# An opening with sums ahead of factors, and a second sweep whose weights are split two products ahead

## The chip, the cores and the metric

The kernel runs on one core of a Trainium2 chip. The metric is the time of one execution on the device in microseconds (us). The core has a matrix engine (PE), a vector engine (DVE), a scalar engine (ACT) and GpSimd (POOL); SP issues most loads. Each engine executes its own instructions in a fixed order and waits where an operand isn't there.

## The reference

One block of a streaming encoder, in float32, for 1024 tokens of 2048 channels:

```python
mod = einsum('bd,de->be', silu(c), w_ada) + b_ada          # shift, scale, gate
h = rms_norm(x, g_pre) * (1 + scale) + shift
q, f, i, z, bb, cc, vb, zb = split(einsum('bsd,de->bse', h, w_in))   # 8 x 1024 columns
f = lb + (1 - lb) * sigmoid(f); k = 1 - f
o = hgrn2_chunkwise(q, log(f), k, i)       # 8 heads of 128, chunks of 64 tokens
y_a = rms_norm(o, g_head_a) * silu(z)
y_b = bb * causal_conv(cc * vb, conv_w, conv_b) * silu(zb)          # 3 taps
m_a, m_b = split(sigmoid(einsum('bsd,de->bse', h, w_merge) + b_merge))
out = einsum('bse,ed->bsd', m_a * (y_a @ w_up_a) + m_b * (y_b @ w_up_b), w_o)
x + gate * rms_norm(out, g_post)
```

## The kernel before

Every large matrix product is done by Strassen's scheme in Winograd's form: seven products p1 to p7 in place of eight, on sums of blocks. Each operand is split into a high and a low float32r half (`hi` on ACT, `lo = raw - hi` on DVE), and each block product is three matmuls (lines 118, 121, 122: hi hi, hi lo, lo hi). A product of the two sweeps has 8 factors, so 24 matmuls of 128x128 by 128x512.

**Opening.** x is loaded, normalised and transposed. Then for four pairs of factors (q = 0 to 3) `ada_pair(q)` loads 16 blocks of w_ada and sums them weighted with silu(c): the scale on PE, the shift on DVE (`row_v`, 16 operations). `factors_a` then applies scale and shift to the transposed x (ACT), forms p1, p6, p2 and p7's right factors and splits them (tiles `fp`, lines 134 and 135).

**First sweep** (`unit_a`, 48 units: 8 heads of 4, then 16 of gates): products p1, p6, p2, p7 of each unit. Partial sums go to DRAM (`u_scr`, `s_scr`). `factors_b`, `gate_step` and `sums_o` are strewn in.

**Second sweep** (`unit_b`, 48 units): p5, p4, p3 of each unit. A head's units bring q and f, v and z, bb and cc, vb and zb. Behind each unit stands the work that its results allow: `Head.f` (Sigmoid, Ln, scans, four Exp), `q`, `v`, `z`, `scores`, `k_nat`, `states`, `o`, `conv` and `norm` (whose Ln and Exp stand on lines 583 and 587). y of each branch goes to `y_scr`.

**up_b, up_a, out.** `up` forms the factors of y (`yp`, 28 of them), and does 8 steps (`du`) of seven products with 4 factors each. Then the last product with w_o.

The program's order is set by a list scheduler that runs when the kernel is built: it takes the text as priority, and puts each engine's instructions in the order in which its own model has them ready. Tiles are taken from pools: `wp` (`w_hi`, `w_lo` two buffers each, raw weights five), `big` (38 tiles of 512 KB) and a pool for the phase, `ph0` to `ph4`; a phase's tiles lie where those of the phase before lay, and wait for their last use.

Of the kernel before, what the change touches and what calls it, by code (L numbers as in the profile page):

```python
# [26 lines left out]
def tile_hgrn2_shortconv_block(  # L27
# [288 lines left out]
    def unit_a(u):  # L316
        view, e1, e2 = units[u]
        a11, a21 = load_q(view, 0, e1), load_q(view, 0, e2)
        a22, a12 = load_q(view, 1, e2), load_q(view, 1, e1)
        o = ph.tile([P, 3, HS], F32, tag="o", name="o", bufs=2)  # L320
        s1, s2, s4 = (ph.tile([P, 8, P], F32, tag=f"s{n}", name=f"s{n}") for n in (1, 2, 4))
        px, py = ps("mm", "px"), ps("mm", "py")
        product(px, split_w(a11), fa["p1"], pin=u == 0)
# [56 lines left out]
    for u in range(NU):  # L380
        unit_a(u)
        if u < 8:
            factors_b(u)
        elif u < 40:
            gate_step(u - 8)
        else:
            sums_o(u - 40)
# [11 lines left out]
    d_ring = []  # L399
    d_n = [0]  # L400

    def d_tile():
# [4 lines left out]
        return t

    def unit_b(u):
# [8 lines left out]
        pz, pw = ps("mm", "pz"), ps("mm", "pw")  # L418
        product(pz, split_w(s1), fb["p5"])
        nc.vector.tensor_add(out=d2[:, hi_h], in0=d2[:, lo_h], in1=pz)  # L420
        product(pw, split_w(a22), fb["p4"])
        nc.vector.tensor_sub(out=d2[:, lo_h], in0=d2[:, lo_h], in1=pw)
        product(pz, split_w(s4), fb["p3"], more=True)
        nc.vector.tensor_add(out=d1[:, hi_h], in0=d1[:, hi_h], in1=pz)
        return d1, d2
# [42 lines left out]
    class Head:
# [3 lines left out]
        def f(self, sig):  # L472
# [47 lines left out]
        def scores(self):  # L520
            px = [ps("aux", "sc0"), ps("aux", "sc1")]
            for blk in range(8):
                hf, c0 = blk // 4, (blk % 4) * P
                t0, t1 = slice(blk * P, blk * P + CH), slice(blk * P + CH, blk * P + P)
                lo, up = px[hf][0:CH], px[1 - hf][CH:P]
                first, last = blk % 4 == 0, blk % 4 == 3
                nc.tensor.matmul(lo[:, c0:c0 + CH], self.e2[:, t0], self.e1[:, t0], start=first, stop=False, skip_group_check=True)
                nc.tensor.matmul(up[:, c0 + CH:c0 + P], self.e2[:, t1], self.e1[:, t1], start=first, stop=last, skip_group_check=True)
                nc.tensor.matmul(lo[:, c0 + CH:c0 + P], self.e3[:, t0], self.eb[:, t1], start=False, stop=last, skip_group_check=True)
            for hf in range(2):  # L530
                nc.vector.copy_predicated(out=sc_buf[hf][0:CH].rearrange("p a b -> p (a b)"),
                                          mask=cmask[0:CH].rearrange("p a b -> p (a b)"), data=px[hf][0:CH])
# [59 lines left out]
    def conv(ct, d_bb, d_cc, d_vb, d_zb):  # L592
        u = ph.tile([P, S + 2], F32, tag="u", name="u")
        nc.gpsimd.memset(u[:, 0:2], 0.0)
        nc.vector.tensor_mul(out=u[:, 2:S + 2], in0=d_cc, in1=d_vb)
        y = wide("y")
        nc.vector.tensor_scalar(out=y, in0=u[:, 0:S], scalar1=cw_c[:, ct:ct + 1], scalar2=cb_c[:, ct:ct + 1], op0=mult, op1=add)
        for j in (1, 2):
            nc.vector.scalar_tensor_tensor(out=y, in0=u[:, j:j + S], scalar=cw_c[:, j * 8 + ct:j * 8 + ct + 1], in1=y, op0=mult, op1=add)
        nc.vector.tensor_mul(out=y, in0=y, in1=d_bb)  # L600
        nc.vector.tensor_mul(out=y, in0=y, in1=d_zb)
        nc.scalar.activation(out=d_zb, in_=d_zb, func=AF.Sigmoid)
        nc.vector.tensor_mul(out=y, in0=y, in1=d_zb)
        nc.gpsimd.dma_start(out=y_scr[8 + ct], in_=y)

    for i in range(NH):
        hd = Head(i)
        d_q, d_f = unit_b(4 * i)
        hd.f(d_f)
        hd.q(d_q)  # L610
        d_v, d_z = unit_b(4 * i + 1)
        hd.v(d_v)
        hd.z(d_z)
        hd.scores()
        d_bb, d_cc = unit_b(4 * i + 2)
        hd.k_nat()
        hd.states()
        d_vb, d_zb = unit_b(4 * i + 3)
        hd.o()
        conv(i, d_bb, d_cc, d_vb, d_zb)  # L620
        hd.norm()

    for m in range(16):
        for j, t in enumerate(unit_b(32 + m)):
            et = 2 * m + j
            nc.scalar.activation(out=t, in_=t, func=AF.Sigmoid, bias=bm_c[:, et:et + 1])
            nc.gpsimd.dma_start(out=g_scr[et], in_=t)
# [249 lines left out]
```

## Time and profile before

| | us |
|---|---|
| median of 3 runs (lowest, highest) | 2820.7 (2820.16, 2821.09) |
| profiled execution, its span | 2822.96, 2821.3 |
| PE busy | 2668.6 (95%) |
| DVE busy | 1740.5 (62%) |
| ACT busy | 952.8 (34%) |

Busy times of the engines overlap. In the trace the opening lasts to the first matmul of unit 0 at 147 us, the first sweep to 1229, the second to 2160, and the rest to the end. PE's times are those of matmuls in a pipeline, so one matmul's 0.39 us overlaps the next one's. PEclk is the TensorE clock that was granted, as a share of 2.4 GHz.

### The profile page before, as it was taken

Reading aid. Unit: us, or ns where it says so; the run is one execution under the profiler, and the core shown is the slowest. Engines: PE = TensorE matmul, PEld = TensorE weight load, DVE = VectorE, ACT = ScalarE, POOL = GpSimd, SP = SyncE. Lnnn points to the kernel's source line nnn. Section 1 sums busy time; section 2 is a strip of 40 time slices with the busy share of each in tenths; the row PEclk is TensorE's granted clock in tenths of the full one; section 3 lists DMA queues with packets and bytes.
Section 4 is the critical chain, followed back from the end, with each engine's and each line's share of the span. In section 5 each row is a group of like instructions: output and inputs, shape, how many; then the busy total and the mean of one; then the engine's idle time right before and its main releaser. Section 6 shows DMA issues by size and latency. Waiting matters only on the chain.

```text
span 2821.3 us, 31341 instructions
## 1 busy us (share of the span) xinstructions
PE 2668.6 (95%) x11979; PEld 2147.0 (76%) x11979; DVE 1740.5 (62%) x2141; ACT 952.8 (34%) x1208; POOL 241.3 (9%) x430
## 2 busy tenths in 40 slices
PE   6779999999999999999999999999999999999997
PEld 3167787888888888877877777877887877878785
DVE  6778876654554445546556666563338678755668
ACT  5333222222222222234335544434334233232334
POOL 2012111110000000020000000000001101000000
PEclk9789999999999999999999999999999999999999
DMA  9759999985556566683433433447666546672254
GB/s 352 276 192 326 333 346 354 345 277 176 177 194 177 175 174 181 187 293 121 127 123 123 135 127 113 137 160 235 204 207 210 179 142 239 219 278 98 85 213 168
DMA packets 405991, 576.77 MB, mean 204 GB/s; under 512 B 17772, under 2 KB 280016, under 8 KB 405712
## 3 DMA queue, kind: packets, MB, share of 16 engines
q1 hardware_dynamic: 352640, 369.15, 42.4%
q0 software_dynamic: 52016, 201.42, 18.8%
q10 hardware_dynamic: 1184, 4.20, 0.4%
q8 instruction: 94, 1.54, 0.2%
q14 instruction: 57, 0.47, 0.1%
HBM read 405.87 MB, written 168.82 MB: 204 GB/s over the span
## 4 chain that ended last, share of the span: by engine, by line
PE 78%; DVE 8%; ACT 5%; DMA 4%; issue 4%; POOL 1%; DVEq 0%; SPq 0%; POOLq 0%; ACTq 0%
PE po L766 9%; PE py L122 7%; PE py L118 7%; PE py L121 7%; PE px L122 6%; PE px L121 6%; PE px L118 6%; PE pz L118 6%; PE pz L121 6%; PE pz L122 6%; PE pw L122 3%; PE pw L118 3%; PE pw L121 3%; DVE w_lo L130 1%; DMA w_raw<-in_w_in_dram 1%
## 5 line engine op out<-in xcount | busy, mean ns | idle before, releaser
L129 ACT CAST w_hi<-w_raw 128x1024 fp32r<-128x1024 f32 (+1 forms) x304 | 299.3, 985 | 979.1 <-PE px L121 382.8
L130 DVE TENSOR_TENSOR w_lo<-w_raw,w_hi 128x1024 fp32r<-128x1024 f32 (+1 forms) x304 | 349.2, 1149 | 256.1 <-ACT w_hi L129 252.1
L122 PE MATMUL pz<-fp,w_lo 128*128 128x512 f32 x768 | 301.8, 393 | 11.4 <-DVE w_lo L130 11.4
L118 PE MATMUL px<-fp,w_hi 128*128 128x512 f32 x768 | 299.4, 390 | 7.9 <-ACT fp L134 7.9
L118 PE MATMUL py<-fp,w_hi 128*128 128x512 f32 x768 | 301.2, 392 | 5.2 <-DVE o L329 5.2
L122 PE MATMUL py<-fp,w_lo 128*128 128x512 f32 x768 | 303.4, 395 | 1.9 <-DVE w_lo L130 1.7
L121 PE MATMUL px<-fp,w_hi 128*128 128x512 f32 x768 | 299.6, 390 | 5.6 <-DVE fp L135 5.6
L118 PE MATMUL pz<-fp,w_hi 128*128 128x512 f32 x768 | 301.4, 392 | 0.2 <-ACT w_hi L129 0.2
L122 PE MATMUL px<-fp,w_lo 128*128 128x512 f32 x768 | 300.3, 391 | 1.2 <-DVE w_lo L130 1.2
L121 PE MATMUL py<-fp,w_hi 128*128 128x512 f32 x768 | 301.0, 392 | 0.0
L121 PE MATMUL pz<-fp,w_hi 128*128 128x512 f32 x768 | 299.3, 390 | 0.0
L766 PE MATMUL po<-w_hi,lt 128*128 128x512 f32 x896 | 245.8, 392 | 6.2 <-ACT lt L134 4.0
L129 ACT CAST w_hi<-s_raw 128x1024 fp32r<-128x1024 f32 x96 | 100.7, 1049 | 356.0 <-PE pw L121 181.4
L766 PEld LDWEIGHTS po<-w_hi,lt 128*128 128x128 f32 x896 | 168.7, 189 | 44.4 <-ACT lt L134 4.8
L122 PE MATMUL pw<-fp,w_lo 128*128 128x512 f32 x384 | 157.2, 409 | 32.4 <-DVE w_lo L130 32.4
L129 ACT CAST w_hi<-s 128x512 fp32r<-128x512 f32 (+1 forms) x112 | 90.1, 805 | 274.2 <-PE py L121 244.5
L122 PEld LDWEIGHTS pz<-fp,w_lo 128*128 128x128 f32 x768 | 144.2, 188 | 44.8 <-DVE w_lo L130 14.9
L122 PEld LDWEIGHTS py<-fp,w_lo 128*128 128x128 f32 x768 | 145.5, 189 | 37.7 <-DVE w_lo L130 7.2
L118 PEld LDWEIGHTS px<-fp,w_hi 128*128 128x128 f32 x768 | 144.4, 188 | 39.1 <-ACT fp L134 9.0
L118 PEld LDWEIGHTS py<-fp,w_hi 128*128 128x128 f32 x768 | 145.5, 189 | 36.3 <-issue 6.5
L121 PEld LDWEIGHTS px<-fp,w_hi 128*128 128x128 f32 x768 | 144.2, 188 | 36.3 <-DVE fp L135 6.4
L121 PEld LDWEIGHTS py<-fp,w_hi 128*128 128x128 f32 x768 | 145.6, 190 | 30.9
(278 smaller groups left out, 4584.2 us busy)
## 6 DMA issues: line engine op xcount, KB each, us to landing
w_raw<-in_w_in_dram SPq DMA_DIRECT2D x160, 512.0 KB, 5.1
s_scr<-s POOLq DMA_DIRECT2D x96, 512.0 KB, 6.1
s_raw<-s_scr SPq DMA_DIRECT2D x96, 512.0 KB, 4.4
w_raw<-in_w_merge_dram SPq DMA_DIRECT2D x80, 512.0 KB, 5.4
u_scr<-o POOLq DMA_DIRECT2D x48, 768.0 KB, 7.3
ada_raw<-in_w_ada_dram SPq DMA_DIRECT2D x64, 512.0 KB, 7.7
d<-u_scr SPq DMA_DIRECT2D x48, 512.0 KB, 3.6
ga_raw<-in_w_ada_dram SPq DMA_DIRECT2D x32, 512.0 KB, 8.7
```

The source lines that it names most:

```text
L118: mm = nc.tensor.matmul(o, ah, bh, start=first, stop=False, skip_group_check=True)
L121: nc.tensor.matmul(o, ah, bl, start=False, stop=False, skip_group_check=True)
L122: nc.tensor.matmul(o, al, bh, start=False, stop=last, skip_group_check=True)
L129: nc.scalar.copy(out=hi, in_=raw)
L130: nc.vector.tensor_sub(out=lo, in0=raw, in1=hi.bitcast(F32))
L766: nc.tensor.matmul(o, a, b[:, c], start=st, stop=sp, skip_group_check=True)
```

## The change

Opening: `ada_pair(q)` comes ahead of `factors_a` of the pair before; `factors_a` takes both factors of a pair at once, goes stage by stage, and for factor 7 applies scale and shift on DVE. In unit 0, p1 and p6 run first on factors 0 to 5 and then on 6 and 7. `factors_b`, `gate_step` and `sums_o` are called in other units.

Second sweep: the products of all units form one list; weights are split two products ahead, with a third buffer (`hi3`, `lo3`) that p3 always takes. The work on heads and convolution is cut into pieces that are called one after each product, a unit later than before. y of the convolution uses the tile `lf`. `scores` makes a block of 128x128 where three of 64x64 stood, with the one cross block of 64x64 in a bank of its own.

```diff
...
-    def product(o, w, f, more=False, pin=False):
+    def product(o, w, f, more=False, pin=False, gs=None):
         n = len(f)
-        for g in range(n):
-            mm3(o, w[0][:, g], w[1][:, g], f[g][:, 0], f[g][:, 1], g == 0 and not more, g == n - 1, pin and g == 0)
+        for g in gs or range(n):
+            mm3(o, w[0][:, g], w[1][:, g], f[g][:, 0], f[g][:, 1], g == 0 and not more, g == n - 1, pin)
...
+    def factors_a(gs, vec=()):
+        parts = []
+        for g in gs:
...
+            for o, i, k in ((he, he, ke), (b22, ho[:, hi_h], ko), (b21, b21, ko)):
+                if g in vec:
+                    nc.vector.tensor_scalar(out=o, in0=i, scalar1=a_c[:, k:k + 1], scalar2=sh_c[:, k:k + 1], op0=mult, op1=add)
+                else:
+                    nc.scalar.activation(out=o, in_=i, func=AF.Identity, scale=a_c[:, k:k + 1], bias=sh_c[:, k:k + 1])
+            parts.append((g, b11, b12, b21, b22))
...
+        for g, b11, b12, b21, b22 in parts:
+            keep_f("p1", g, b11)
+        for g, b11, b12, b21, b22 in parts:
+            nc.vector.tensor_sub(out=b12, in0=b22, in1=b12)
+            nc.vector.tensor_add(out=b11, in0=b12, in1=b11)
+            keep_f("p6", g, b11)
...
-    for q in range(4):
+    ada_pair(0)
+    for q in range(1, 4):
         ada_pair(q)
-        factors_a(2 * q)
-        factors_a(2 * q + 1)
+        factors_a((2 * q - 2, 2 * q - 1))
+    factors_a((6, 7), vec=(7,))
...
-        product(px, split_w(a11), fa["p1"], pin=u == 0)
+        w1 = split_w(a11)
+        if u:
+            product(px, w1, fa["p1"])
...
+        if u == 0:
+            for gs in (range(6), (6, 7)):
+                product(px, w1, fa["p1"], pin=True, gs=gs)
+                product(py, w6, fa["p6"], pin=True, gs=gs)
...
+        if u < 16:
+            if u % 2 == 0:
+                factors_b(u // 2)
+        elif u < 32:
+            gate_step(2 * u - 32)
+            gate_step(2 * u - 31)
+        elif u % 2 == 0:
+            sums_o((u - 32) // 2)
...
+    third = (ph.tile([P, 8, P], F32R, name="hi3"), big.tile([P, 8, P], F32R, tag="big", name="lo3"))
+    n_b = [0]
+
+    def split_b(raw):
+        n_b[0] += 1
+        return split_w(raw, out_t=third if n_b[0] % 3 == 0 else None)
...
-                lo, up = px[hf][0:CH], px[1 - hf][CH:P]
-                first, last = blk % 4 == 0, blk % 4 == 3
-                nc.tensor.matmul(lo[:, c0:c0 + CH], self.e2[:, t0], self.e1[:, t0], start=first, stop=False, skip_group_check=True)
-                nc.tensor.matmul(up[:, c0 + CH:c0 + P], self.e2[:, t1], self.e1[:, t1], start=first, stop=last, skip_group_check=True)
-                nc.tensor.matmul(lo[:, c0 + CH:c0 + P], self.e3[:, t0], self.eb[:, t1], start=False, stop=last, skip_group_check=True)
+                nc.tensor.matmul(px[hf][:, c0:c0 + P], self.e2[:, bs], self.e1[:, bs], start=blk % 4 == 0, stop=blk % 4 == 3, skip_group_check=True)
+                nc.tensor.matmul(pc[0:CH, blk * CH:(blk + 1) * CH], self.e3[:, t0], self.eb[:, t1], start=blk == 0, stop=blk == 7, skip_group_check=True)
...
+            y = self.y = wide("lf")
...
+        i, j = u // 4, u % 4
+        if j == 0:
+            hd = now["hd"] = Head(i)
+            later.extend([lambda: hd.f(d2), hd.f2, lambda: (hd.f3(), hd.q(d1))])
+            return
+        hd = now["hd"]
+        if j == 1:
+            later.extend([lambda: hd.v(d1), lambda: hd.z(d2), hd.scores])
+        elif j == 2:
+            now["cv"] = Conv(i, d1, d2)
+            later.extend([hd.k_nat, hd.states])
+        else:
+            cv = now["cv"]
+            later.extend([lambda: cv.first(d1), lambda: (cv.last(d2), hd.o()), hd.norm])
+
+    seq = [(u, s) for u in range(NU) for s in ("p5", "p4", "p3")]
+    ready, loaded = [], {}
+
+    def ahead(n):
+        if n < len(seq):
+            u, s = seq[n]
+            if s == "p5":
+                loaded[u] = load_b(u)
+            ready.append(split_b(loaded[u][s]))
+
+    ahead(0)
+    ahead(1)
+    for n, (u, s) in enumerate(seq):
+        ahead(n + 2)
+        w = ready.pop(0)
...
+        if later:
+            later.pop(0)()
+        if s == "p3":
+            done(u, d1, d2)
...
```

How this moves instructions is shown at three places. First ACT where a head of the second sweep begins. Before (`r` belongs to the old head's norm, `d` and `lf` to the new head's gate f, `e` and `b` to its exponentials, `w_hi` to the next products):

```order
L506 COPY vn<-pk 128x512
L474 ACT_TABLE_LOAD
L474 ACTIVATE d_8330<-d_8330 128x1024
L477 ACT_TABLE_LOAD
L477 ACTIVATE lf<-d_8330,lbt 128x1024
L129 CAST w_hi<-w_raw 128x1024
L485 ACT_TABLE_LOAD
L485 ACTIVATE e_8305<-e_8305 128x1024
L486 ACTIVATE e_8303<-e_8304 128x1024
L488 ACTIVATE b<-b 128x1024
L487 ACTIVATE e_8304<-e_8304 128x1024
L129 CAST w_hi<-s_raw 128x1024 x2
```

After the change, at the same place (`zs` belongs to a gate of the new head):

```order
L129 CAST hi_8175<-s_raw 128x1024
L492 ACT_TABLE_LOAD
L492 ACTIVATE lf<-d_8625,lbt 128x1024
L605 ACTIVATE r<-pss,eps_t 128x512
L609 ACT_TABLE_LOAD
L609 ACTIVATE r<-r 128x512
L605 ACT_TABLE_LOAD
L605 ACTIVATE r<-pss,eps_t 128x512
L609 ACT_TABLE_LOAD
L609 ACTIVATE r<-r 128x512
L129 CAST w_hi<-s_raw 128x1024
L505 ACTIVATE e_8208<-e_8208 128x1024
```

The new head's Ln (line 492) comes ahead of the old head's norm (lines 605 and 609), the four Exp behind it, and casts for products further ahead (`hi3`, then `w_hi`) stand between.

Next DVE in the opening, from the first sums of pair 1 on. Before (`row_v` are the sums, `fp` the factors):

```order
L236 TENSOR_SCALAR row_v<-ada_raw,c_act 128x512
L238 SCALAR_TENSOR_TENSOR row_v<-ada_raw,c_act,row_v 128x512
L246 TENSOR_TENSOR a_c<-pa,cols 128x4
L248 TENSOR_TENSOR sh_c<-pa,cols 128x4
L247 SCALAR_TENSOR_TENSOR a_c<-a_c,cols 128x4
L269 TENSOR_TENSOR xT_416<-keep_735,xT_416 128x512
L269 TENSOR_TENSOR xT_430<-keep_735,xT_430 128x512
L135 TENSOR_TENSOR fp_0_739<-xT_416,fp_0_739 128x512
L270 TENSOR_TENSOR xT_416<-xT_416 128x512
L135 TENSOR_TENSOR fp_0_744<-xT_416,fp_0_744 128x512
L135 TENSOR_TENSOR fp_0_747<-xT_423,fp_0_747 128x512
L135 TENSOR_TENSOR fp_0_750<-xT_416,fp_0_750 128x512
```

After:

```order
L236 TENSOR_SCALAR row_v<-ada_raw,c_act 128x512
L238 SCALAR_TENSOR_TENSOR row_v<-ada_raw,c_act,row_v 128x512 x5
L246 TENSOR_TENSOR a_c<-pa,cols 128x4
L248 TENSOR_TENSOR sh_c<-pa,cols 128x4
L238 SCALAR_TENSOR_TENSOR row_v<-ada_raw,c_act,row_v 128x512
L247 SCALAR_TENSOR_TENSOR a_c<-a_c,cols 128x4
L238 SCALAR_TENSOR_TENSOR row_v<-ada_raw,c_act,row_v 128x512 x3
L277 TENSOR_TENSOR xT_416<-keep_815,xT_416 128x512
L238 SCALAR_TENSOR_TENSOR row_v<-ada_raw,c_act,row_v 128x512 x3
L277 TENSOR_TENSOR xT_430<-keep_815,xT_430 128x512
L238 SCALAR_TENSOR_TENSOR row_v<-ada_raw,c_act,row_v 128x512
L135 TENSOR_TENSOR fp_0_822<-xT_416,fp_0_822 128x512
```

The sums of pair 1 now run on between the factor operations of pair 0, instead of behind all of them.

Last DVE where up_b's factors (`yp`, from `y` and the sums `t`) are formed. Before, with units 45 and 46 (`d` are results of the second sweep; lines 420 to 424 take them from PSUM):

```order
L149 TENSOR_TENSOR t_14176<-y_14149,y_14147 128x512
L150 TENSOR_TENSOR y_14147<-y_14149,y_14147 128x512
L680 TENSOR_TENSOR s_14285<-w_raw 128x512
L420 TENSOR_TENSOR d_8330<-d_8330,pz 128x512
L130 TENSOR_TENSOR w_lo<-s_raw,w_hi 128x1024
L135 TENSOR_TENSOR yp_1_14166<-y_14151,yp_1_14166 128x512
L147 TENSOR_TENSOR y_14151<-y_14151 128x512
L149 TENSOR_TENSOR t_14183<-y_14153,y_14151 128x512
L150 TENSOR_TENSOR y_14151<-y_14153,y_14151 128x512
L676 TENSOR_TENSOR s_14283<-w_raw 128x512
```

After, from the result of unit 47's p4 (line 685) to that of its p3 (line 688) and on:

```order
L150 TENSOR_TENSOR y_14095<-y_14097,y_14095 128x512
L150 TENSOR_TENSOR y_14099<-y_14101,y_14099 128x512
L685 TENSOR_TENSOR d_13934<-d_13934,pw 128x512
L130 TENSOR_TENSOR w_lo<-w_raw,w_hi 128x512
L149 TENSOR_TENSOR t_14116<-y_14089,y_14087 128x512
L149 TENSOR_TENSOR t_14123<-y_14093,y_14091 128x512
L743 TENSOR_TENSOR s_14223<-w_raw 128x512
L747 TENSOR_TENSOR s_14225<-w_raw 128x512
L688 TENSOR_TENSOR d_13933<-d_13933,pz 128x512
L135 TENSOR_TENSOR yp_0_14119<-t_14116,yp_0_14119 128x512
L744 TENSOR_TENSOR s_14224<-s_14223,w_raw 128x512
L135 TENSOR_TENSOR yp_1_14126<-t_14123,yp_1_14126 128x512
```

The first sum `t` for p6 (line 149) stood some 45 DVE instructions ahead of the last p3's result before the change and stands four ahead of it now; it waits there for the last p3 matmul of unit 47, as `t` now lies on `hi3`. From it to the low half of the last p3 factor of up_b there are 53 DVE instructions.

## Rows read from the trace of the kernel before

**Rows 1.** Waits of PE in the second sweep: total us, times, longest us.

```profile
PE pw L122 <- DVE w_lo L130: 32.4, 8, 4.6
PE pz L122 <- DVE w_lo L130: 11.4, 8, 1.4
```

**Rows 2.** Windows of two heads: window, us, busy by engine, PEclk, DMA share, GB/s.

```profile
1312.00:1396.00 84.00, 78.00 (x403) 64.50 (x403) 51.70 (x62) 38.03 (x39) 4.60 (x8) 0.98 0.39 125
1396.00:1480.00 84.00, 78.00 (x399) 64.43 (x398) 50.63 (x60) 38.02 (x39) 4.40 (x6) 0.96 0.39 125
```

**Rows 3.** Timeline of ACT where a head begins: start us, us, instruction, [idle before].

```profile
1405.50 1.28 ACT L587 ACT_TABLE_LOAD   x1
1406.79 0.63 ACT L587 ACTIVATE r<-r 128x512 f32<-128x512 f32 x1
...
1408.86 1.28 ACT L474 ACT_TABLE_LOAD   x1
...
1412.53 1.24 ACT L477 ACTIVATE lf<-d,lbt 128x1024 f32<-128x1024 f32 x1
```

**Rows 4.** Timeline of DVE at the same place.

```profile
1407.46 0.75 DVE L588 SCALAR_TENSOR_TENSOR r<-po,cols,r 128x512 f32<-128x512 f32 x1 [2.12 <-ACT r L587]
...
1409.32 1.22 DVE L130 TENSOR_TENSOR w_lo<-s_raw,w_hi 128x1024 fp32r<-128x1024 f32 x1
1413.81 0.81 DVE L478 TENSOR_SCALAR d<-d,noml,lbt 128x1024 f32<-128x1024 f32 x1 [3.27 <-ACT lf L477]
...
1418.50 1.22 DVE L484 TENSOR_TENSOR e<-b 128x1024 f32<-128x1024 f32 x1
1419.64 1.22 DVE L130 TENSOR_TENSOR w_lo<-w_raw,w_hi 128x1024 fp32r<-128x1024 f32 x1
```

**Rows 5.** Timeline of PE in a head's score matmuls.

```profile
1439.88 0.27 PE L527 MATMUL sc<-e,e 128*64 128x64 f32 x1
...
1441.68 0.28 PE L529 MATMUL sc<-b,e 128*64 128x64 f32 x2
```

**Rows 6.** Instructions of line L545 in one head: min/median/max ns, first and last start.

```profile
L545 PE MATMUL pd<-vn,e x14: 270/275/275, 1454.0 to 1455.5; 128*128 128x128 f32 x14
```

**Rows 7.** Windows of 10 us in the opening, columns as in rows 2.

```profile
70.00:80.00 10.00, 10.00 (x23) 1.94 (x22) 8.83 (x14) 3.40 (x7) 0.00 (x0) 0.93 1.02 377
80.00:90.00 10.00, 6.63 (x25) 3.29 (x23) 7.05 (x12) 1.24 (x2) 0.00 (x0) 0.76 0.50 161
```

**Rows 8.** Timeline of DVE in the opening, at two pairs' ends and in one pair.

```profile
58.35 0.48 DVE L236 TENSOR_SCALAR row_v<-ada_raw,c_act 128x512 f32<-128x512 f32 x1 [0.63 <-DMA ada_raw<-in_w_ada_dram]
...
76.00 10.98 DVE L238 SCALAR_TENSOR_TENSOR row_v<-ada_raw,c_act,row_v 128x512 f32<-128x512 f32 x14
...
147.55 0.16 DVE L246 TENSOR_TENSOR a_c<-pa,cols 128x4 f32<-128x4 f32 x1 [1.70 <-PE pa L243]
```

**Rows 9.** Timeline of PE in unit 0 of the first sweep.

```profile
161.05 0.80 PE L121 MATMUL px<-fp,w_hi 128*128 128x512 f32 x1 [4.82 <-DVE fp L135]
...
176.61 0.39 PE L118 MATMUL px<-fp,w_hi 128*128 128x512 f32 x1
176.84 0.39 PE L121 MATMUL px<-fp,w_hi 128*128 128x512 f32 x1
```

**Rows 10.** DMA issues: transfer, queue, count, KB each, median us to landing.

```profile
g_scr<-d POOLq DMA_DIRECT2D x32, 512.0 KB, 5.6
...
xr<-in_x_dram POOLq DMA_DIRECT2D x16, 512.0 KB, 13.2
y_scr<-y POOLq DMA_DIRECT2D x8, 512.0 KB, 3.8
```

**Rows 11.** Timeline of PE at the start of up_b and of its second step.

```profile
2160.20 0.50 PE L118 MATMUL px<-yp,w_hi 128*128 128x512 f32 x1
...
2186.40 0.39 PE L118 MATMUL px<-yp,w_hi 128*128 128x512 f32 x1
```

**Rows 12.** Timeline of DVE in up_b.

```profile
2173.61 3.10 DVE L135 TENSOR_TENSOR yp<-y,yp 128x512 fp32r<-128x512 f32 x5
```

More of the change, by code (lines that the diff above doesn't have):

```diff
@@ L381, in tile_hgrn2_shortconv_block @@
         unit_a(u)
[L382 to L387, printed above, removed]
+        if u < 16:
[6 more added lines that the diff above has]
+            sums_o((u - 32) // 2)
     ph_pool.__exit__(None, None, None)
@@ L417, in unit_b @@
         nc.sync.dma_start(out=d1.rearrange("p (a b) -> p a b", a=2), in_=u_scr[u][:, 0:2])
[L418 to L425, printed above, removed]
+        return {"p5": s1, "p4": a22, "p3": s4, "d": (d1, d2)}
     scan_m = ph.tile([P, HS], F32, name="scan_m")
@@ L463, in wide @@
         return slots[tag]
+    for tag in ("lf", "b", "e1", "e2", "e3", "vn", "zs"):
+        wide(tag)
     def small(name, dt=F32):
@@ L590, in norm @@
             nc.gpsimd.dma_start(out=y_scr[self.hd], in_=self.zs)
[L592 to L627, printed above, removed]
+    class Conv:
+        def __init__(self, ct, d_bb, d_cc):
+            self.ct, self.bb, self.cc = ct, d_bb, d_cc
+        def first(self, d_vb):
+            ct = self.ct
+            u = ph.tile([P, S + 2], F32, tag="u", name="u")
+            nc.gpsimd.memset(u[:, 0:2], 0.0)
+            nc.vector.tensor_mul(out=u[:, 2:S + 2], in0=self.cc, in1=d_vb)
+            y = self.y = wide("lf")
+            nc.vector.tensor_scalar(out=y, in0=u[:, 0:S], scalar1=cw_c[:, ct:ct + 1], scalar2=cb_c[:, ct:ct + 1], op0=mult, op1=add)
+            for j in (1, 2):
+                nc.vector.scalar_tensor_tensor(out=y, in0=u[:, j:j + S], scalar=cw_c[:, j * 8 + ct:j * 8 + ct + 1], in1=y, op0=mult, op1=add)
+        def last(self, d_zb):
+            y = self.y
+            nc.vector.tensor_mul(out=y, in0=y, in1=self.bb)
+            nc.vector.tensor_mul(out=y, in0=y, in1=d_zb)
+            nc.scalar.activation(out=d_zb, in_=d_zb, func=AF.Sigmoid)
+            nc.vector.tensor_mul(out=y, in0=y, in1=d_zb)
+            nc.gpsimd.dma_start(out=y_scr[8 + self.ct], in_=y)
@@ new lines, in tile_hgrn2_shortconv_block, with done, gates @@
+    later = []
+    now = {}
+    def done(u, d1, d2):
+        if u >= 32:
+            def gates():
+                for j, t in enumerate((d1, d2)):
+                    et = 2 * (u - 32) + j
+                    nc.scalar.activation(out=t, in_=t, func=AF.Sigmoid, bias=bm_c[:, et:et + 1])
+                    nc.gpsimd.dma_start(out=g_scr[et], in_=t)
+            later.append(gates)
+            return
[3 more added lines that the diff above has]
+            later.extend([lambda: hd.f(d2), hd.f2, lambda: (hd.f3(), hd.q(d1))])
+            return
+        hd = now["hd"]
[7 more added lines that the diff above has]
+            later.extend([lambda: cv.first(d1), lambda: (cv.last(d2), hd.o()), hd.norm])
@@ new lines, in tile_hgrn2_shortconv_block @@
+    seq = [(u, s) for u in range(NU) for s in ("p5", "p4", "p3")]
[11 more added lines that the diff above has]
+        w = ready.pop(0)
+        d1, d2 = loaded[u]["d"]
+        if s == "p5":
+            pz, pw = ps("mm", "pz"), ps("mm", "pw")
+            product(pz, w, fb[s])
+            nc.vector.tensor_add(out=d2[:, hi_h], in0=d2[:, lo_h], in1=pz)
+        elif s == "p4":
+            product(pw, w, fb[s])
+            nc.vector.tensor_sub(out=d2[:, lo_h], in0=d2[:, lo_h], in1=pw)
+        else:
+            product(pz, w, fb[s], more=True)
+            nc.vector.tensor_add(out=d1[:, hi_h], in0=d1[:, hi_h], in1=pz)
+        if later:
+            later.pop(0)()
+        if s == "p3":
+            done(u, d1, d2)
@@ L628, in tile_hgrn2_shortconv_block @@
+    for f in later:
+        f()
     ph_pool.__exit__(None, None, None)
```

61 lines of the change are left out of this document (29 added, 32 removed).

## The prediction

> **What bounds the kernel now.** PE is busy for 95% of the span, so first I listed where it waits, over the whole span and then stage by stage. In the first sweep it waits little after unit 0. In the second sweep nearly all of its waiting has one name, `w_lo`, the low half of a split weight tile: 43.8 us in 16 waits, half of them long (up to 4.6 us) and half short (1.4 us) [rows 1]. Seven of each fall where a new head begins, in heads 2 to 8; the next two paragraphs are about those.
>
> The timelines of ACT and DVE at such a place tell why. ACT runs the old head's last exponential behind a table load, then table load, Sigmoid, table load, Ln for the new head [rows 3]. DVE's gain waits 2.12 us for that exponential, and the first `w_lo` stands behind it; the next DVE instruction waits 3.27 us for Ln, and the second `w_lo` comes behind it, two scans and two subtractions, at 1419.64, although its `w_hi` was there long before [rows 4]. PE has weights for only one product ahead, so it stops for both. The third view is the windows: those seven heads were granted a clock of 0.98 (three of them) or 0.96 (four) [rows 2], that is a stretch at 1.2 GHz instead of 2.4 after the stop. Lost by it: 84 x (3 x 0.02 + 4 x 0.04) = 18.5 us.
>
> In the opening the sums of a pair (DVE) and its factors (ACT, then DVE) take turns. The first pair's sums end at 58.35 - 0.63 = 57.7, the last one's at 147.55 - 1.70 = 145.85 [rows 8]: 88.1 us for three pairs, 29.4 each, of which 16 sums by 10.98/14 = 0.78 are only 12.5. While factors run, buffers stay full and loads stop: 377 GB/s in one 10 us window, 161 in the next [rows 7]. Then unit 0 waits for factors 6 and 7, product by product (one wait of 4.82), and its third product starts at 176.6, 30.8 us after the last sum [rows 9].
>
> **The change, part by part.**
>
> *Opening, pairs.* With factors one pair late, DVE fills the time. A pair then costs DVE 12.5 for sums and 12 factor operations by 3.10/5 = 0.62 [rows 12], 7.4: 19.9 us. Loads: 16 x 0.524 MB = 8.4 MB, at 377 GB/s 22.3 us, so DMA sets the pace. The best window isn't held throughout; I take 24.4, and the last sum at 57.7 + 3 x 24.4 = 131: **-15**. Bounds: 22.3 gives 125 (-21); half of the old dips left gives 138 (-8).
>
> *Opening, tail.* Products 1 and 6 now both run on factors 0 to 5, then on 6 and 7. What stands on DVE between the last sum and the low half of the last p6 factor is 1.7 of waiting and 0.5 of column operations, nine 128x1024 operations by 1.14 (start to start in [rows 4]) and eight or so 128x512 by 0.62: 17.5 to 18 us; three or four more operations until the third product's `w_lo`: 22 us, against 30.8. **-9** (bounds -4 and -10: weights for unit 1 may come late and hold DVE's queue). The three factor operations moved to DVE are in that sum. Opening: **-24**, which I round to -23 for a clock that rises later.
>
> *Middle of the first sweep.* factors_b, gate steps and sums_o are spaced otherwise in the text, but the scheduler starts their loads at about the old places: 0 (-4 to +4).
>
> *Heads.* Splits two products ahead take the `w_lo` waits away if the new order is in time. The order shows the tightest place, told here for head 2 (units 4 to 7): PE's first matmul of unit 6's p5 now stands before unit 5's p3. From the start of unit 4's p3, PE gets there after three products of 24 x 0.23 = 5.5 us [rows 9] and four matmuls of the norm by at most 0.23 ([rows 6]: 13 record starts over 1.5 us, two records each), at 17.3. ACT gets there after `hi3` (which must wait until p3 has read the old one, about 5.2, then at most 1.24), four table loads by 1.28, Ln 1.24, four activations on r by 0.63 and the cast, at most 1.24: 6.4 + 5.1 + 1.2 + 2.5 + 1.2 = 16.4 [rows 3]. Margin 0.9 us, thin; elsewhere it is over 1 us. So 43.8 + 18.5 = 62.3 us go, and I put back 5 for waits that remain. Behind the late cast stand the exponentials, and behind these DVE's `w_lo`.
>
> A table load is charged here with what its row has: 1.28 us, and the next instruction starts 0.01 behind it [rows 3]. The Trainium skill, "ScalarE: Activation LUTs", What ACT_TABLE_LOAD costs, adds a drain of 1.38 us to each load; by that the cast would be 4 x 1.38 = 5.5 us later. This case's trace shows no such time, and the sum goes by the trace.
>
> *A new wait in the heads.* y of the convolution lies in tile `lf`, so the next head's Ln waits until y is stored. That store is issued about when p3 of unit 4 starts and lands in 3.8 [rows 10]; Ln is due at 6.4. Covered, with 2.6 to spare plus the 0.9 above.
>
> *Scores.* 24 matmuls of 64x64 took 1441.68 + 0.28 - 1439.88 = 2.1 us, 0.087 each, since pairs overlap [rows 5]. Now 8 of 128x128, by 0.23 [rows 6], and 8 of 64x64, by 0.087 to 0.23: 2.5 to 3.7. **+4** for 8 heads (+3 to +13), on PE's path. Four fewer table loads a head save ACT 5.1 us, but ACT bounds nothing there; the two copies of scores take some of it.
>
> Second sweep: -62.3 + 5 + 4 = **-53**.
>
> *Transition to up_b.* The new tile `hi3` takes room in the phase pool, and the next phase's `t` and `s` tiles lie on it. So the p6 factors of y, which DVE made early before, now wait until the last p3 matmul of unit 47. In the order 53 DVE operations then stand between that point and the last factor of the first step. At 0.62 each plus 2 of waiting: 35 us. Before, PE's first step ran from 2160.2 to 2186.4, 26.2 us [rows 11]. **+8** (bounds: +4, if later steps' products fill the gaps; +13, if ACT's casts are late too). PE waits in this time, so its clock hardly counts.
>
> Sum: -23 + 0 - 53 + 8 = **-68** on the profiled execution's 2823.0 (span 2821.3 and 1.7 around it): 2755. The runs' median is 2.3 lower: **2753**.
>
> **The rivals.**
>
> 1. *As above*: 2753, own range 2742 to 2765. Chance 0.56.
> 2. *No price at the transition and heads with no wait at all*: 8 and 5 less, 2740. For it: later steps' matmuls are ready and independent. Against: the order puts 53 operations in one queue. 0.13.
> 3. *The opening gives little*: loads, not turns, set the pairs' pace, and unit 0 waits for weights as before: -8 and -2 instead of -23, 2766. For it: DMA share is 1.02 at its best [rows 7]. 0.13.
> 4. *The heads keep one wait*, because ACT's chain at the tight place is 3 us longer than my sum (the norm's matmuls wait for POOL's casts): 2 us a head, and about 2.3 of slow clock behind it (18.5/8), 8 x 4.3 = 34 less 5 already counted: 2782. 0.12.
> 5. *A table load stops ACT for longer than its row*, with as much again before it: 4 x 1.28 = 5.1, the cast misses by 4.2, and 8 x (4.2 + 2.3) - 5 = +47: 2800. Against it: the rows leave 0.01 us there. 0.02. (The skill's page named above says that there is such a time.)
> 6. *Slower*: the store of y holds Ln. It decides in every head, at L492, once the landing exceeds 3.8 + 3.5 = 7.3 us; each microsecond beyond costs 8, and each head 2.3 for the clock. To eat all 68 it takes (68 + 5 - 8 x 2.3)/8 = 6.8 more, a landing of 14.1. The slowest transfer of this size lands in 13.2, a store of gates in 5.6 [rows 10]. With two or three such stores in a queue it could be 15: 2828. 0.02.
> 7. *The change doesn't do what it says*, since the scheduler moves the splits back: 2821. The order shows them two ahead, so 0.02.
>
> **How the numbers follow.** A measurement of this kernel tells 0.2%, 5.6 us, from no change. Rivals 1 to 5 are faster by more, 0.96; I leave 0.94 for what isn't on my list, 0.02 for the same and 0.04 for slower. The range for 8 in 10 reaches to rivals 2 and 4 with their bounds: 2732 (all terms at their better bounds give -23 - 7 - 4 - 58 + 4 = -88) to 2786.
>
> **What would show it.** Right: no wait for `w_lo` over 1 us in heads 2 to 8 and a clock of 1.0 in their windows; heads 76 to 77 us apart instead of 84; the last sum near 131 and unit 0's third product near 153; PE waits for factors of y after the second sweep, and the first step of up_b lasts about 35 us. Wrong: PE waiting on `w_hi` or on Ln's chain in each head, windows with a clock under 1, pairs still 29 us apart, or a second sweep of more than 890 us.

## The result, and the profile after

The changed kernel takes 2787.4 us (median of 4 runs, 2786.26 to 2790.2) against 2820.9 before (4 runs): ratio 0.988 with a 95% interval of 0.986 to 0.990, so faster by 1.2%, 33.5 us. Half of the 68 us forecast came, and the time lies 1.4 us above the range.

By stage, in the profiled executions (2821.3 before, 2784.6 after: -36.7):

| us | before | after | change | forecast |
|---|---|---|---|---|
| start of the second sweep | 1229.4 | 1212.8 | -16.6 | -23 |
| second sweep, to its last matmul | 930.3 | 904.5 | -25.8 | -53 |
| first step of up_b | 26.5 | 33.3 | +6.8 | +8 |
| the rest | 635.1 | 634.0 | -1.1 | 0 |

The waits of PE in the second sweep, as in [rows 1], hold no `w_lo` any more; a new one stands there, once in each of seven heads:

```profile
PE pk L529 <- DVE d L688: 11.0, 7, 2.1
```

The windows of two heads, 80.4 us each and no longer 84, show the full clock where [rows 2] had 0.98 and 0.96, and PE idle for 1.2 to 1.5 us. Of the seven heads that begin behind another, six show the full clock. The third line is the window of the other one, where the new wait is longest: PE was idle for 2.06 us, and just behind that, in the window of the fourth line, the granted clock was 0.50, that is 1.2 GHz:

```profile
1298.00:1378.40 80.40, 78.87 (x387) 65.17 (x386) 49.92 (x59) 33.03 (x38) 5.23 (x7) 1.00 0.40 131
1378.40:1458.80 80.40, 79.16 (x389) 65.45 (x389) 50.18 (x60) 33.31 (x38) 5.24 (x7) 1.00 0.41 132
...
1619.60:1700.00 80.40, 78.34 (x374) 64.35 (x373) 47.75 (x57) 32.23 (x37) 5.22 (x7) 0.98 0.39 125
...
1656.00:1658.00 2.00, 2.00 (x6) 1.54 (x5) 0.97 (x1) 0.00 (x0) 0.00 (x0) 0.50 0.50 128
```

So the old waits went, as forecast, and the low clock with them but for that one head; and something else lengthens each head. PE's timeline in the scores of one head, beside [rows 5]:

```profile
1423.16 0.38 PE L551 MATMUL sc<-e,e 128*128 128x128 f32 x2
1423.47 0.33 PE L552 MATMUL scx<-b,e 128*64 128x64 f32 x2
1423.73 0.49 PE L551 MATMUL sc<-e,e 128*128 128x128 f32 x2
1424.15 0.33 PE L552 MATMUL scx<-b,e 128*64 128x64 f32 x2
1424.40 0.49 PE L551 MATMUL sc<-e,e 128*128 128x128 f32 x2
...
1428.46 0.50 PE L118 MATMUL pz<-fp,w_hi 128*128 128x512 f32 x1
```

From the first score matmul to the next product it takes 5.3 us, in all eight heads; the 24 small ones of before took 2.0, counted the same way. A pair of one wide and one narrow block comes every 0.67 us (1423.73 to 1424.40), and nothing is waited for: a view of waits cannot show this.

The new wait, followed back at the start of a head. The tile `zs` holds the old head's gate, normed and stored, and then the new head's. First the last instructions on that tile there (min/median/max ns, first and last start), then the timelines of POOL, ACT, DVE and PE:

```profile
L611 DVE TENSOR_TENSOR zs<-zs,r x1: 680/680/680, 1400.8 to 1400.8; 128x512 f32<-128x512 f32 x1
L612 POOL DMA_DIRECT2D y_scr<-zs x1: 587/587/587, 1403.9 to 1403.9; - x1
```

```profile
1401.09 1.56 POOL L515 COPY dec<-b 128x16 f32<-128x16 f32 x1 [17.57 <-ACT b L508]
1402.74 1.24 POOL L518 TENSOR_TENSOR decp<-dec 128x8 f32<-128x8 f32 x1
1403.92 0.59 POOL L612 DMA_DIRECT2D y_scr<-zs  x1
```

```profile
1397.08 1.03 ACT L129 CAST w_hi<-s_raw 128x1024 fp32r<-128x1024 f32 x1
...
1408.40 1.28 ACT L541 ACT_TABLE_LOAD   x1 [5.54 <-DMA y_scr<-zs]
1409.69 1.06 ACT L541 ACTIVATE zs<-d 128x1024 f32<-128x1024 f32 x1
```

```profile
1410.79 1.23 DVE L542 TENSOR_TENSOR zs<-zs,d 128x1024 f32<-128x1024 f32 x1 [4.00 <-ACT zs L541]
1411.93 0.68 DVE L688 TENSOR_TENSOR d<-d,pz 128x512 f32<-128x512 f32 x1
```

```profile
1398.97 0.39 PE L118 MATMUL pz<-fp,w_hi 128*128 128x512 f32 x1
...
1412.66 0.66 PE L529 MATMUL pk<-ident,d 128*128 128x128 f32 x4 [1.25 <-DVE d L688]
```

The old head's `zs` is ready at 1400.8 + 0.68 = 1401.5. Its store stands on POOL behind two small operations of the new head, is issued at 1403.92 and lands at 1408.40. Until then ACT can't write the new head's `zs`; DVE's multiplication waits for ACT, `d` stands behind it, and PE's transposes need `d`.

The tight place of the prediction is the cast into `w_hi` at 1397.08. It ended at 1398.11, 0.86 ahead of PE's use at 1398.97. This is head 3, and the widest of the seven margins. In head 2, for which the prediction told it, the margin was 0.48 where 0.9 was forecast, and in the others 0.3 to 0.6:

```profile
1317.11 1.03 ACT L129 CAST w_hi<-s_raw 128x1024 fp32r<-128x1024 f32 x1
...
1318.62 0.39 PE L118 MATMUL pz<-fp,w_hi 128*128 128x512 f32 x1
```

Part of the margin went to the store of y. It took 6.1 us to land, not the 3.8 of [rows 10], and Ln's table load waited for it in six of the seven heads. These are the row of the transfer, and ACT's wait (total us, times, longest us):

```profile
y_scr<-lf POOLq DMA_DIRECT2D x8, 512.0 KB, 6.1
ACT L492 <- DMA y_scr<-lf: 2.3, 6, 0.6
```

The opening, in windows as in [rows 7], and DVE's timeline as in [rows 8]:

```profile
50.00:60.00 10.00, 6.86 (x16) 1.18 (x14) 7.36 (x10) 0.00 (x0) 0.00 (x0) 1.00 1.05 387
60.00:70.00 10.00, 0.00 (x0) 0.00 (x0) 0.00 (x0) 0.00 (x0) 0.00 (x0) 0.56 1.05 387
70.00:80.00 10.00, 7.35 (x23) 2.61 (x24) 6.22 (x12) 1.53 (x2) 0.00 (x0) 0.67 0.75 265
80.00:90.00 10.00, 10.00 (x23) 1.93 (x22) 9.89 (x16) 7.43 (x12) 0.00 (x0) 0.92 0.49 158
```

```profile
54.57 3.12 DVE L238 SCALAR_TENSOR_TENSOR row_v<-ada_raw,c_act,row_v 128x512 f32<-128x512 f32 x4
73.32 0.49 DVE L236 TENSOR_SCALAR row_v<-ada_raw,c_act 128x512 f32<-128x512 f32 x1 [15.64 <-DMA ada_raw<-in_w_ada_dram]
...
133.26 3.90 DVE L238 SCALAR_TENSOR_TENSOR row_v<-ada_raw,c_act,row_v 128x512 f32<-128x512 f32 x5
```

For 10 us DMA moves 387 GB/s and no engine does anything: the bytes arrive in the wrong order. The last block of pair 0, one for the scale, comes late, behind eleven blocks of pair 1 (so the program's order on SP has it), and PE waits 15.1 us for it:

```profile
PE prow L234 <- DMA ada_raw<-in_w_ada_dram: 20.7, 4, 15.1
```

DVE's wait of 15.64 us above is for the block that stands right behind it on SP, the first for the shift of pair 1. Once the eleven have filled the buffers, the loads fall to 158 GB/s. The last sum ends at 133.26 + 3.90 = 137.2, where it was 145.85 before.

Behind it, PE in unit 0: the third product's first `w_lo` matmul is 21.3 us behind the last sum (forecast 22; before, 30.8 to its very first matmul [rows 9]).

```profile
158.47 0.50 PE L122 MATMUL px<-fp,w_lo 128*128 128x512 f32 x1 [0.52 <-DVE w_lo L130]
```

### The profile page after: what moved, and what is told of

Its sections match the earlier page's. It is cut to its first block, busy times and chain, and to the rows that moved or that the text cites. A ratio compares the mean times of both kernels' runs of the same rounds, so it can differ in the third digit from the quotient of the medians.

```text
span 2784.6 us, 31067 instructions
## 1 busy us (share of the span) xinstructions
PE 2670.7 (96%) x11851; PEld 2152.5 (77%) x11851; DVE 1725.3 (62%) x2128; ACT 915.0 (33%) x1192; POOL 246.6 (9%) x431
## 4 chain that ended last, share of the span: by engine, by line
PE 71%; issue 11%; DVE 7%; DMA 6%; ACT 3%; POOL 2%; DVEq 0%; POOLq 0%; ACTq 0%; SPq 0%
PE po L833 9%; PE py L122 6%; PE py L121 6%; PE px L122 6%; PE py L118 6%; PE px L118 6%; PE px L121 6%; PE pz L118 5%; PE pz L122 5%; PE pz L121 5%; PE pw L121 3%; PE pw L122 3%; PE pw L118 3%; DMA w_raw<-in_w_in_dram 2%; DVE w_lo L130 1%
## 5 line engine op out<-in xcount | busy, mean ns | idle before, releaser
L122 PEld LDWEIGHTS px<-fp,w_lo 128*128 128x128 f32 x768 | 144.4, 188 | 37.1 <-DVE w_lo L130 7.0
L118 PE MATMUL pz<-fp,hi 128*128 128x512 f32 x384 | 151.8, 395 | 0.0
L121 PE MATMUL pw<-fp,w_hi 128*128 128x512 f32 x384 | 151.4, 394 | 0.0
L118 PE MATMUL pw<-fp,w_hi 128*128 128x512 f32 x384 | 151.0, 393 | 0.0
L118 PE MATMUL pz<-fp,w_hi 128*128 128x512 f32 x384 | 150.4, 392 | 0.0
L122 PE MATMUL pw<-fp,w_lo 128*128 128x512 f32 x384 | 150.1, 391 | 0.0
```

The costliest lines, as they stand in the source:

```text
L118: mm = nc.tensor.matmul(o, ah, bh, start=first, stop=False, skip_group_check=True)
L121: nc.tensor.matmul(o, ah, bl, start=False, stop=False, skip_group_check=True)
L122: nc.tensor.matmul(o, al, bh, start=False, stop=last, skip_group_check=True)
```

## Experiments

Each ran beside the kernel before, which took 2821.9 to 2822.6 there. Differences from the changed kernel are against its median of 2787.4.

**1. The scores alone.** The kernel before with the new `scores` and nothing else of the change. For each of 8 blocks these two matmuls stand in place of three of 64x64:

```diff
+                nc.tensor.matmul(px[hf][:, c0:c0 + P], self.e2[:, bs], self.e1[:, bs], start=blk % 4 == 0, stop=blk % 4 == 3, skip_group_check=True)
+                nc.tensor.matmul(pc[0:CH, blk * CH:(blk + 1) * CH], self.e3[:, t0], self.eb[:, t1], start=blk == 0, stop=blk == 7, skip_group_check=True)
```

> The kernel before, with nothing of the change but the new score matmuls (8 of 128x128 and 8 of 64x64 in turn, and their copies). Theory A, that PE loses time at each change between a 128-wide and a 64-wide matmul: the scores take 5.3 us a head as in the changed kernel instead of 2.1, 8 x 3.2 = +26 us, 2846. Theory B, the prediction's price of the matmuls alone: +4 (to +13), 2825 to 2834. Theory C, that the 5.3 us come from what surrounds the scores in the changed kernel (busy banks, the copies on ACT): 2821 to 2825.

Measured: 2849.3, ratio 1.010 [1.0085, 1.0115], 27.4 us slower. The scores take 5.3 us a head, and the waits are those of [rows 1] to 0.1 us:

```profile
PE pw L122 <- DVE w_lo L130: 32.3, 8, 4.6
PE pz L122 <- DVE w_lo L130: 11.5, 8, 1.4
```

So one edit of the change costs 8 x 3.3 = 26 us by itself, where the forecast had 4.

**2. The same matmuls, grouped.** All eight wide blocks first, then all eight narrow ones:

```diff
                 nc.tensor.matmul(px[hf][:, c0:c0 + P], ...
+            for blk in range(8):
+                t0, t1 = slice(blk * P, blk * P + CH), slice(blk * P + CH, blk * P + P)
                 nc.tensor.matmul(pc[0:CH, blk * CH:(blk + 1) * CH], ...
```

> The changed kernel, with all eight 128x128 score matmuls ahead of all eight 64x64 ones, so that the kind changes twice a head instead of 16 times. Theory A: 8 x 0.23 + 8 x 0.09 and two changes, 2.6 to 3.0 us a head instead of 5.3: -18 to -22 us, 2766 to 2769. Theory B (each matmul costs what it costs in any order): 2784 to 2788. A third way, that the copies wait longer for the last matmul: no more than +1 a head, 2795.

Measured: 2769.7, 17.7 less than the changed kernel (0.981 [0.980, 0.983] of before). PE's timeline, one head:

```profile
1420.33 1.95 PE L551 MATMUL sc<-e,e 128*128 128x128 f32 x16
1422.21 1.15 PE L554 MATMUL scx<-b,e 128*64 128x64 f32 x16
1423.28 0.50 PE L118 MATMUL pz<-fp,w_hi 128*128 128x512 f32 x1
```

The same 16 matmuls take 2.95 us. Alternating changes width 15 times between them, grouped once: (5.31 - 2.95)/14 = 0.17 us a change.

**3. All of one width, still alternating.** The narrow block computes 128 rows, of which half go unused:

```diff
-                nc.tensor.matmul(pc[0:CH, blk * CH:(blk + 1) * CH], self.e3[:, t0], ...
+                nc.tensor.matmul(pc[:, blk * CH:(blk + 1) * CH], self.e3[:, bs], ...
```

> The changed kernel, with the cross block made 128 wide too: eight matmuls of 128x64 in the place of 64x64, still in turn with the 128x128 ones. Half of their rows are not used; the output is the same. Theory A, that the width is what costs when it changes: no change any more, 8 x 0.23 + 8 x 0.12 to 0.19, 2.8 to 3.4 us a head instead of 5.3: -15 to -20 us, 2767 to 2772. Rival, that it is the turn itself (two operands, two banks, two weight tiles): 5.3 or more, 2787 to 2792.

Measured: 2771.3, 16.1 less than the changed kernel; 3.49 us a head, with more rows computed than in the slow form. PE's timeline, one head:

```profile
1417.18 0.44 PE L551 MATMUL sc<-e,e 128*128 128x128 f32 x2
1417.46 0.33 PE L552 MATMUL scx<-b,e 128*128 128x64 f32 x2
1417.63 0.44 PE L551 MATMUL sc<-e,e 128*128 128x128 f32 x2
```

A pair comes every 0.45 us instead of 0.67. The turn between two banks and two tiles is as before, and the work is more. So at least 5.31 - 3.49 = 1.8 us a head, 0.12 for each of the 15 changes, comes with the change between 128 and 64 columns of weights.

**4. The old scores in the changed kernel.**

```diff
-                nc.tensor.matmul(px[hf][:, c0:c0 + P], self.e2[:, bs], self.e1[:, bs], ...
-                nc.tensor.matmul(pc[0:CH, blk * CH:(blk + 1) * CH], self.e3[:, t0], ...
+                nc.tensor.matmul(lo[:, c0:c0 + CH], self.e2[:, t0], self.e1[:, t0], ...
+                nc.tensor.matmul(up[:, c0 + CH:c0 + P], self.e2[:, t1], self.e1[:, t1], ...
+                nc.tensor.matmul(lo[:, c0 + CH:c0 + P], self.e3[:, t0], self.eb[:, t1], ...
```

> The changed kernel, with the scores of before (24 matmuls of 64x64) and its copies. Theory A (a change between 128 and 64 wide costs some 0.2 us each, 16 a head): the scores take 2.1 us again: 8 x 3.2 = -26 us, 2760 to 2763. Rival, that the copies of before (four on DVE, of 64 partitions) hold something now: -15 to -20.

Measured: 2765.6, 21.8 less (0.981 [0.979, 0.982]), between the two expectations; 2.01 us a head. All 24 are 64 wide, and are the fastest form of the four. The `pk` wait stays (11.9 us). In the trace the second sweep is 24.2 shorter (880.3 against 904.5), and what stands behind the first step of up_b is 2.5 longer (636.5 against 634.0).

**5. The norm's result elsewhere.** It goes into `vn`, which the new head needs much later, and is stored from there:

```diff
-                nc.vector.tensor_mul(out=zs, in0=zs, in1=r)
-            nc.gpsimd.dma_start(out=y_scr[self.hd], in_=self.zs)
+                nc.vector.tensor_mul(out=self.vn[:, halves[hf]], in0=zs, in1=r)
+            nc.gpsimd.dma_start(out=y_scr[self.hd], in_=self.vn)
```

> The changed kernel, with the norm's last product written to tile vn instead of zs and stored from there, so that the next head's Sigmoid into zs needn't wait for that store. Theory: the store of zs holds ACT (5.5 us at the second head), ACT holds DVE's product on zs, behind which the result stands that PE's transposes wait for; all seven waits of 1.3 to 2.1 us go: -11 us, 2776. Rival: PE stands too early in its own order for that result whatever ACT does; the waits stay: 2787. Second rival: the copies into vn now wait for the store instead: 2787 to 2795.

Measured: 2772.0, 15.4 less (0.982 [0.980, 0.984]). The seven waits are gone, and the sweep lasts 890.4 instead of 904.5. So the store held them: its landing takes no engine's time, only the tile. The gain is more than the 11.0 us of the waits. Some 1.4 of the rest was the stretch at 1.2 GHz, which went too: seven matmuls in a row had come 0.43 us apart there and not 0.23.

**6. Loads of w_ada in the order of their use.** Every third load takes one of four buffers of its own, and so waits until PE or DVE has read the block in it; after the first twelve, now all take a freed tile of `big`:

```diff
-        if n_ada[0] % 3:
+        if n_ada[0] > 12 or n_ada[0] % 3:
             raw = bigt(F32, "ada_raw").rearrange("p (k e) -> p k e", k=2)
```

> The changed kernel, with the ring of four buffers for w_ada used in pair 0 alone until its fourth load; all other loads take big tiles, and SP issues all 64 in the order in which they are used. Theory: the 15 us in which PE and DVE do nothing at 58 to 73 us come from SP's order, in which eleven loads of pair 1 stand ahead of pair 0's last; they go, loads run on at 387 GB/s, and the last sum ends at 57.7 + 3 x 21.7 to 23 = 123 to 127 instead of 137: -10 to -14 us, 2773 to 2777. Rival: DMA's rate sets the whole, and what comes early for pair 1 is lost nowhere: -2 to +2, 2787.

Measured: 2774.9, 12.5 less (0.983 [0.981, 0.985]). The windows at the place of the idle stretch, and DVE's last sum:

```profile
60.00:70.00 10.00, 9.62 (x33) 2.98 (x33) 5.70 (x12) 5.97 (x8) 0.00 (x0) 1.00 1.05 386
70.00:80.00 10.00, 6.85 (x17) 1.02 (x15) 9.94 (x16) 4.15 (x8) 0.00 (x0) 1.00 1.05 387
80.00:90.00 10.00, 8.93 (x32) 2.83 (x31) 8.69 (x15) 5.33 (x7) 0.00 (x0) 1.00 1.05 386
```

```profile
122.48 2.32 DVE L238 SCALAR_TENSOR_TENSOR row_v<-ada_raw,c_act,row_v 128x512 f32<-128x512 f32 x3
```

The last sum ends at 124.8, 12.4 earlier. With the dip and the idle stretch gone DMA sets the pace of the pairs, near the forecast's better bound (125).

**7. `hi3` in `big`, and `zs` in the phase pool in its place.**

```diff
-    third = (ph.tile([P, 8, P], F32R, name="hi3"), big.tile(...
+    third = (big.tile([P, 8, P], F32R, tag="big", name="hi3"), big.tile(...
-            slots[tag] = bigt(F32, tag)
+            slots[tag] = ph.tile([P, S], F32, name="zs") if tag == "zs" else bigt(F32, tag)
```

> The changed kernel, with hi3 in the pool big and zs in the phase pool in its place, so that the next phase's first tiles don't lie on hi3. Theory of the transition's price: the p6 factors of y are formed before the last p3 ends, the first step of up_b takes 26 to 28 us instead of 33, -5 to -7 us, 2780 to 2782. Rival: DVE is behind by as much anyway, since it does the gates' results one unit later: -2 to +1.

Measured: 2781.5, 5.9 less (0.986 [0.984, 0.987]). The first step of up_b lasts 28.1 us instead of 33.3; before the change it was 26.5. So what the factors of y waited for was the tile under them, as read from the order, for 5.2 of the 6.8 us.

**8. Experiments 4 to 7 together.**

> The changed kernel with four edits together: the scores of before, the norm's result in vn, w_ada loads in the order of use, hi3 in big. If the four causes are separate, the sum of the parts: 2787 - 26 - 15 - 12.5 - 6 = 2727.5 (2722 to 2735). If two of them hide behind the same wait, 2735 to 2750.

Measured: 2730.6, ratio 0.968 [0.966, 0.969] of before: the best version, 3.2% faster than before and 56.8 us under the changed kernel. The parts measured apart give 21.8 + 15.4 + 12.5 + 5.9 = 55.6. The one wait of PE in the second sweep, and windows of two heads:

```profile
PE pz L118 <- DVE d L683: 0.7, 1, 0.7
```

```profile
1270.00:1345.60 75.60, 75.60 (x403) 63.29 (x402) 51.11 (x61) 33.74 (x36) 5.23 (x7) 1.00 0.42 140
1345.60:1421.20 75.60, 75.60 (x402) 63.33 (x401) 51.04 (x62) 32.47 (x35) 5.23 (x7) 1.00 0.43 140
```

PE is busy throughout, 75.6 us a head. With 3.3 for the scores and 11.0/7 = 1.6 for the wait that is the changed kernel's 80.4.

**9. Is it the splits two ahead?** The text asks for weights one product ahead, the third buffer stays:

```diff
-    ahead(1)
     for n, (u, s) in enumerate(seq):
-        ahead(n + 2)
+        ahead(n + 1)
```

> The changed kernel, with the list of products asking for weights one product ahead instead of two, and the third buffer kept. ACT's order at a head's start comes out as in the changed kernel, so if the scheduler's order and the buffers are what counts, nothing changes: 2785 to 2790. Rival, that the two in the text is what takes the waits for w_lo away: they return, up to +50.

Measured: 2787.1, 0.3 less: no change. In the two traces ACT's and DVE's instructions of the sweep come in the same order. The scheduler, with a buffer to spare, puts the splits where they stood; so this tells nothing of the buffer, nor of weights asked for later.

**10. One ahead, and no third buffer.** As 9, and

```diff
-        return split_w(raw, out_t=third if n_b[0] % 3 == 0 else None)
+        return split_w(raw)
```

> As the run before, and without the third buffer: all products take w_hi and w_lo in turn, two buffers each. Theory: the third buffer is what lets casts stand ahead of a head's Ln and Exp; without it PE waits for w_lo or w_hi in each head again, though the norm's Ln and Exp lie elsewhere: 3 to 6 us a head with the slow clock behind, +25 to +45, 2812 to 2832. Rival, that the pieces' new places suffice: under +10.

Measured: 2788.2, 0.8 more: a miss, and the rival's number. The waits in the sweep:

```profile
PE pz L122 <- DVE w_lo L130: 11.2, 9, 1.4
PE pk L529 <- DMA d<-u_scr: 5.0, 1, 5.0
```

The long `w_lo` waits of up to 4.6 us [rows 1] do not come back. The short ones do: a wait of 1.4 us a head, 11.2 in all, where [rows 1] had 11.4, takes the place of that for `pk`. With 5.0 more for one load in the first head the sweep is 10.5 us longer; the rest, from its last matmul on, is 5.2 shorter, with a first step of up_b of 26.7, since no `hi3` lies under its tiles. So the third buffer took away the short waits, and not the long ones. For those what is left is the new order of the text: the pieces of work in new places, and weights still asked for one product ahead, where the kernel before asks for them at the product. No run parts these two.

**11. The change up to the end of the first sweep, with the second sweep of before** (its `factors_a`, the order of `ada_pair`, unit 0 and the calls strewn in; diff as in the change).

> The kernel before, with the change up to the end of the first sweep and none of it in the second. By the traces, the second sweep begins 16.6 us earlier in the changed kernel, and nothing behind it should give that back: -15 to -18, 2804 to 2807. Rival, that the second sweep of before loses some of it, since its first loads come at another time: -8 to -14.

Measured: 2807.9 (2804.5 to 2815.3), ratio 0.996 [0.994, 0.997], 14.3 faster than before. It lies between the two expectations, nearer to the profile's 16.6; between them its spread can't decide. One trace doesn't settle it either: in the nine profiled executions with this opening (the changed kernel's, those of experiments 2 to 5, 7, 9 and 10, and this one's) the second sweep starts at 1209.7 to 1216.9 us, and the last of these is this one's.

**12. Experiment 8 without the third buffer** (both edits of 9 and 10).

> The kernel with the four edits, with weights asked for one product ahead and without the third buffer (as in the run with two buffers, where 1.4 us of waiting for w_lo a head stood in the place of the transposes' waits). Theory, that the third buffer pays once the other wait is gone: 8 x 1.4 = +11 (+8 to +16), 2739 to 2747. Rival, that it pays nothing here either: 2728 to 2734.

Measured: 2759.4, 28.8 more than experiment 8 (0.978 [0.976, 0.980] of before): the right sign, at 2.6 times the size and beyond the range expected. Waits in the sweep, and windows of two heads:

```profile
PE pz L122 <- DVE w_lo L130: 15.3, 14, 1.7
PE pk L528 <- DMA d<-u_scr: 4.8, 1, 4.8
```

```profile
1270.00:1349.10 79.10, 76.95 (x411) 63.70 (x410) 51.48 (x62) 33.74 (x36) 3.92 (x7) 1.00 0.42 134
1349.10:1428.20 79.10, 76.64 (x403) 63.10 (x402) 50.90 (x62) 32.38 (x35) 4.03 (x7) 1.00 0.42 133
```

A head is 3.5 us longer: 2.2 to 2.5 of it is idle time of PE, the `w_lo` waits. In the other 1.0 to 1.4 PE counts as busy at the full clock. Part of it stands beside the waits: at each of a head's two `w_lo` waits, the two matmuls beside it take together some 0.27 us more, from start to start and without the idle time, than the usual 0.23 each. Where the rest goes stays open. Another 4.8 us is one wait for a load in the first head. So the third buffer is worth 28.8 us in this kernel, where nothing else holds the heads. In the changed kernel it was worth next to nothing on balance, 0.8 by the medians; in the traces it saved 10.5 in the sweep and cost 5.2 behind it (experiment 10).

## Why the prediction was wrong, and which of its terms held

**The old waits: right in size, in cause only for the short ones.** The 43.8 us of `w_lo` waits went entirely, and the low clock behind them in six heads of seven. The tight place held, with half the margin that was forecast for head 2 (0.48 of 0.9). The store of y was not "covered, with 2.6 to spare": it landed in 6.1 us and not 3.8, and Ln waited for it by 0.3 to 0.6 us in six heads, which the thin margin just absorbed. And "splits two products ahead take the `w_lo` waits away" holds for the short waits alone: without the third buffer they come back, and the long ones stay away (experiment 10). The 18.5 us for the clock were some 2 too many: of a low stretch of 6.8 us behind a long wait PE was idle for 1.2, and these had been counted as waiting.

**"Scores: +4 (+3 to +13)" is the step that failed most**, by 22 us: it cost 26 by the rows, 27.4 when added to the kernel before, and 21.8 when taken out of the changed kernel. I took the price of a 64-wide matmul between 0.087 and 0.23 from rows in which neighbours have the same width, and no row of before had two widths in turn; the bound held the work and not the turn. The runs show 0.17 us for each of the changes, and none of it with all blocks of 64 columns. The Trainium skill, "TensorEngine Tiling (Array Packing)", Tiling Modes, Key Properties, says that changing the tiling mode drains the matrix engine; it gives no price. The runs agree in that a change costs time, and I had not weighed it; that a drain is what costs it, no run here shows.

**"I put back 5 for waits that remain"**: 11.0 by the view of waits, and 15.4 by the run without them. I priced the store of `lf`, and left out the other store in the same place, that of `zs`. Of the 6.9 us from its data to its landing (1401.5 to 1408.40) it spent 2.4 on POOL's queue, behind the new head's operations.

**Opening, "-15" for the pairs**: 8.7 came, close to the worse bound. That turns of DVE and ACT had held the pace fits the gain; that loads would then flow at DMA's pace was wrong, since SP's order puts a block needed now behind eleven needed later. With that order mended (experiment 6) the better bound came. The tail, the third product 22 us behind the last sum, was right at 21.3.

**Transition, +8**: 6.8, of which experiment 7 takes 5.2 away by moving the tile.

**The range.** The terms that failed were 22 (scores), 6 (the wait in the heads) and 6 (pairs), together 34. Between the profiled executions the miss is 31.3 (-36.7 for -68), as the transition and the rest came out a little better. The medians miss by 34.4, since the changed kernel's lies 1.1 above its profiled execution and not 2.3 below. Heads came 80.4 us apart and not 76 to 77. The second sweep was over the 890 us that the prediction named as its sign of failure, while the missing `w_lo` waits and, but for one head, the clock were its signs of success: both readings held, for different terms. Of the rivals, a head that keeps a wait came true in part (another wait than it named, 1.6 us a head, with its cost in clock in one head of seven), and the opening that gives little in part. None of the rivals had the scores.

## What to carry to other kernels

Look at what stands beside a small matmul, not only at its size: in a long run of products, 16 blocks of two widths in turn took 2.6 times as long as 24 of one width. Where a tile is read by a store and written again, follow the store to its landing on every queue it passes, and give the result a tile that is free for longer. And a spare buffer can seem worth nothing while other costs hide what it saves, so test it again after those are gone.

## What the runs showed of the hardware

A change between 128 and 64 columns of weights cost PE 0.17 us (experiment 2; at least 0.12 by experiment 3), with no wait in the profile and PE counted as busy. A transfer's rate says nothing on whether the right bytes come: 387 GB/s in a 10 us window in which no engine had anything to do. A store of 512 KB from POOL took 6.1 us (`lf`) and 4.4 us (`zs`) to land in the median of eight, and the next write into the tile waited for that in six and in seven of seven heads.
